# Expert inputs gathered in plain float32 by scaled one-hot matrices, four experts at a time, ahead of the experts that use them

## The chip, the core and the metric

The kernel runs on one core of one Trainium2 chip. A core has a tensor engine (TensorE, PE in the rows, its weight loads PEld), a vector engine (VectorE, DVE), a scalar engine (ScalarE, ACT), GpSimd (POOL) and SyncE (SP), whose queue issues most of the transfers. Matrix products are written to PSUM, in banks of 512 float32 per partition; all else lies in SBUF. The metric is the device time of one execution in microseconds (us), the median of several runs; lower is better.

## What is computed

A state-space block is followed by a transformer of two layers (`DEPTH_2 = 2`). The change touches only the feed-forward part of these two layers, in which each of 16 experts picks the 32 of 256 tokens that it rates highest:

```python
def expert_choice_ffn(h, w_router, w1, w3, w2):
    B, T, _ = h.shape
    cap = (EC_CAPACITY_FACTOR * T) // N_EXPERTS          # 32
    aff = jax.nn.softmax((h @ w_router).astype(jnp.float32), axis=-1)
    gate, idx = lax.top_k(jnp.swapaxes(aff, 1, 2), cap)
    bidx = jnp.arange(B)[:, None, None]
    xe = h[bidx, idx]
    hid = jax.nn.silu(jnp.einsum('becd,edf->becf', xe, w1)) * jnp.einsum('becd,edf->becf', xe, w3)
    ye = jnp.einsum('becf,efd->becd', hid, w2) * gate[..., None].astype(h.dtype)
    return jnp.zeros_like(h).at[bidx, idx].add(ye)
```

Here `h` is `rms_norm(x) * (1 + scale) + shift`. In layer 0 this runs on two streams with the same weights, `x` and the context `xc`; in layer 1 on `x` alone. All of `w1`, `w3` and `w2` is 1024 x 1024 float32 per expert, so an expert has 12 MB of weights, and a layer 192 MB.

## The kernel before

`moe(l, streams, stk)` holds the feed-forward of one layer; `ns` is the number of streams, 2 in layer 0 and 1 in layer 1. Its `run()` goes over the experts `e = 0..15` (called expert 0 to 15 here).

**One expert.** `ffn` (L1282) multiplies the expert's gathered inputs by a weight matrix: four tiles `wm` of 1 MB, two blocks `k` of 128 input channels each. In layer 0 one `k` is two products of 64 output columns x 512 (64 = 32 tokens of each stream); they stand in different column halves of the array. In layer 1 one `k` is four products of 32 x 256. The first `ffn` gives `p1`, the second `p3`; `hid` = silu(p1) * p3 is transposed on TensorE (`ps_t`), copied to `hidT`, and the third `ffn` multiplies `hidT` by `w2` into `py`. VectorE multiplies that by `g2` into `ye` (L1349). Every four experts, `gates` builds a matrix `PgT` of gate values, and eight products `ps_b<-ye,PgT` scatter the four experts' outputs back; VectorE adds them to `x` and `xc` (L1361). This is called the combine.

**The gather.** The inputs `xe` of an expert are 1024 channels x 32 tokens, by channel in partitions. `chosen` (L1203) builds a one-hot matrix P (token x chosen slot) by comparing the rank `POS` with `iota1`. `gather(s, part, k)` (L1213) then makes block `k` of stream `s` for all experts of a `part`: the tokens are scaled by `QS` (the 1/rms of each token) and split into two float32r tiles `xp` (ScalarE L1227, VectorE L1228), four products with P add up in one PSUM bank, and `affine` (L160) writes the block to `xe`, ScalarE and VectorE in turn, as (1 + scale) and shift. In layer 0 the parts are experts 0-3, 4-7 and 8-15 (`PARTS`, L1196), in layer 1 four times four experts. There is one buffer of `xp` for the late parts, and in layer 0 two PSUM banks `ps_g` for gathers.

**Order.** The first part is gathered inside expert 0 (`first`); the others are a list `late`, of which `more` takes one item at each of 14 places of an expert. A scheduler of the framework then reorders instructions within engines, by its own simulated times; what stands on an engine is read from the built program, below.

**Weight buffers.** `load_m` (L1268) issues the transfers of `wm` on SP's queue, in the order of use. Each takes the next buffer of a list: 22 in the first round of layer 0 (18 common ones, L1519, and 4 that later become `ye` and the gathered inputs), 18 in each round after it. A transfer waits until the products that read the tile before it in the same buffer are done, and everything behind it on the queue waits too.

Of the kernel before, what the change touches and what calls it, by code (L numbers as in the profile page):

```python
# [113 lines left out]
def kernel(ctx, tc, A, out, dbg=None):  # L114
# [1055 lines left out]
    def moe(l, streams, stk):  # L1170
# [8 lines left out]
        def inputs(part):  # L1179

            if part in xe:
                return
            if part < 2:
                if ns == 2:
                    v = mp.tile([128, 2048], F32, name=("xe0", "xf0")[part])
                else:
                    v = xe["y"][:, 1024:2048] if part else mp.tile([128, 1024], F32, name="xe0")
                v = v.rearrange("p (k e w) -> p k e w", k=8, e=4)
                xe[part] = [v[:, k] for k in range(8)]
            else:  # L1190
                v = [mp.tile([128, 2048], F32, name=f"xf{ns - 1 + i}").rearrange("p (k e w) -> p k e w", k=8 // ns, e=8)
                     for i in range(ns)]
                xe[part] = [v[k * ns // 8][:, k % (8 // ns)] for k in range(8)]


        PARTS = [(0, 4), (4, 4)] + ([(8, 8)] if ns == 2 else [(8, 4), (12, 4)])  # L1196
# [14 lines left out]
        pair = {}  # L1211

        def gather(s, part, k, n=1):  # L1213

            if k % n == 0:
                c = in_pairs(k) if n == 1 else slice(128 * k, 128 * k + 128 * n)
                if n == 1:
                    xp = mp.tile([128, 2, 2, 128], F32R, name="xp")  # L1220
                    h, o = pair[s] = [xp[:, i] for i in range(2)]
                else:
                    h, o = pair[s] = [rowp.tile([128, 512], F32R, name="xp", tag="r").rearrange("p (t c) -> p t c", t=2)
                                      for i in range(2)]
# [4 lines left out]
            e0, ne = PARTS[part]  # L1229
            ps = ps_("g" if ns == 2 else "a")[:, 0:32 * ne].rearrange("p (e w) -> p e w", w=32)  # L1230
# [4 lines left out]
            o = xe[min(part, 2)][k][:, e0 % 8 if part > 1 else 0:][:, :ne]  # L1235
            affine(o[:, :, 32 * s:32 * s + 32], ps, MS[:, i_sc, k, s:s + 1], shift[:, k, s:s + 1])
# [57 lines left out]
        def run():  # L1294
            if ns == 1:
                acc = [psb() for j in range(4)]
# [4 lines left out]
            inputs(0)  # L1301
            P0 = mp.tile([128, ns, 2, 4, 32], F32R, name="P0", tag="P")
            for s in range(ns):
                chosen(s, 0, P0[:, s])

            def first(k):
                for s in range(ns):
                    gather(s, 0, k, 2)
# [556 lines left out]
```

## Time and profile before

| | |
|---|---|
| Median of 3 runs | 1884.86 us (1883.54 to 1889.22) |
| The profiled execution's own time | 1879.31 us |
| Its span, first to last instruction | 1877.3 us |
| Mean granted TensorE clock | 0.928 of full |
| PE, DVE, ACT, POOL busy | 87%, 42%, 28%, 18% of the span |
| HBM read | 554.18 MB, 296 GB/s over the span |
| The chain that ended last | PE 59%, DMA 27%, DVE 7%, ACT 3% |

The span has a first part up to the router of layer 0 (about 755 us), the first expert stage (layer 0, to about 1230 us), layer 1's mixer, and the second expert stage from about 1428 us to the end. The shares are means over stages with different limits. The chain is followed back from the last instruction, at each step to what released it. PEclk is the granted clock, 1.00 for 2.4 GHz and 0.50 for 1.2 GHz. A plain float32 product leaves two records of the same shape in the trace, a float32r product one. A line number is often that of a helper: L149 is every matrix product, L255 every transpose.

### The profile page before, as it was taken

How to read it: one execution, taken by the hardware profiler on the slowest of the kernel's cores; microseconds unless marked ns; L12 is line 12 of the kernel's file. 1: busy time of each engine (PE TensorE's matmuls, PEld its weight loads, DVE VectorE, ACT ScalarE, POOL GpSimd, SP SyncE). 2: the span in 40 equal slices, each digit the busy share in tenths (PEclk: the TensorE clock that was granted, in tenths of full speed). 3: DMA queues.
4: the chain of work that ended last, by engine and by line, in shares of the span. 5: the costliest groups of instructions: out<-in, count | busy, mean ns of one | idle time of the engine just before them, and what ended most of it. 6: DMA issues, size and time to landing. Idle time of an engine off the chain costs nothing.

```text
span 1877.3 us, 29103 instructions
## 1 busy us (share of the span) xinstructions
PE 1642.5 (87%) x12038; PEld 1039.4 (55%) x12038; DVE 788.9 (42%) x1566; ACT 517.8 (28%) x1042; POOL 335.3 (18%) x291
## 2 busy tenths in 40 slices
PE   5999999999999999999989999889997976766665
PEld 4787877889888777433333333258775532222221
DVE  3538889957555665332232121164654410000002
ACT  4334545636444442211110000062442300000001
POOL 4104544733423411000000000031310000000001
PEclk8999999999999999899989999999997987777777
DMA  9567544646576639889969999962187999999996
GB/s 348 189 223 232 167 143 145 201 152 212 179 233 169 228 125 396 313 352 420 421 269 420 421 421 421 420 214 78 68 362 271 423 425 425 425 425 425 425 424 261
DMA packets 173192, 557.13 MB, mean 297 GB/s; under 512 B 22579, under 2 KB 79271, under 8 KB 124164
## 3 DMA queue, kind: packets, MB, share of 16 engines
q1 hardware_dynamic: 166688, 547.92, 75.5%
q10 hardware_dynamic: 5732, 6.33, 1.0%
q8 instruction: 95, 1.56, 0.3%
q0 software_dynamic: 640, 1.02, 0.1%
q14 instruction: 37, 0.30, 0.0%
HBM read 554.18 MB, written 1.05 MB: 296 GB/s over the span
## 4 chain that ended last, share of the span: by engine, by line
PE 59%; DMA 27%; DVE 7%; ACT 3%; issue 2%; POOL 1%; SPq 0%; DVEq 0%; POOLq 0%; ACTq 0%
PE ps_a L149 47%; DMA wm<-in_moe_w_dram 22%; PE ps_b L149 7%; PE ps_b L255 3%; DMA w<-in_w_in_dram 2%; PE ps_g L149 1%; DVE w L827 1%; DMA w<-in_even_w_in_dram 1%; DMA w<-in_w_ada_dram 1%; ACT wh L203 1%; DVE wh L205 1%; DMA w<-in_even_w_out_dram 1%; DVE ye L1349 1%; DVE hid L1331 1%; PE ps_t L255 1%
## 5 line engine op out<-in xcount | busy, mean ns | idle before, releaser
L149 PE MATMUL ps_a<-wm,xf 128*32 128x256 f32 (+1 forms) x1792 | 277.5, 557 | 61.7 <-DMA wm<-in_moe_w_dram 60.3
L149 PE MATMUL ps_a<-wm,hidT 128*32 128x256 f32 (+1 forms) x1536 | 207.2, 509 | 42.0 <-DMA wm<-in_moe_w_dram 25.3
L149 PEld LDWEIGHTS ps_a<-wm,xf 128*32 128x32 f32 (+1 forms) x1792 | 92.5, 138 | 236.3 <-issue 143.3
L203 ACT ACTIVATE wh<-w 128x1024 fp32r<-128x1024 f32 (+3 forms) x152 | 151.6, 1007 | 171.8 <-PE ps_a L149 92.3
L205 DVE TENSOR_TENSOR wh<-w,wh 128x1024 fp32r<-128x1024 f32 (+3 forms) x102 | 135.4, 1331 | 86.5 <-ACT wh L203 86.2
L205 POOL TENSOR_TENSOR wh<-w,wh 128x1024 fp32r<-128x1024 f32 (+3 forms) x50 | 115.0, 2300 | 311.9 <-ACT wh L203 287.8
L1331 DVE TENSOR_TENSOR hid<-hid,ps_a 128x512 f32<-128x512 f32 (+1 forms) x32 | 17.7, 554 | 346.5 <-PE ps_a L149 346.5
L149 PEld LDWEIGHTS ps_a<-wm,hidT 128*32 128x32 f32 (+1 forms) x1536 | 71.3, 131 | 149.2 <-issue 76.5
L1349 DVE TENSOR_TENSOR ye<-ps_a,SC 32x512 f32<-32x512 f32 (+1 forms) x128 | 70.8, 553 | 179.4 <-PE ps_a L149 177.9
L149 PE MATMUL ps_a<-hT,wh 128*128 128x512 f32 (+1 forms) x672 | 138.2, 362 | 5.8 <-ACT hT L522 4.3
L1248 POOL TENSOR_TENSOR Pg<-Pg,BC 128x128 f32<-128x128 f32 x24 | 9.5, 422 | 735.1 <-DVE Pg L1246 735.1
L1329 ACT ACTIVATE hid<-ps_a 128x512 f32<-128x512 f32 (+1 forms) x32 | 15.7, 490 | 448.8 <-PE ps_a L149 448.8
L149 PEld LDWEIGHTS ps_a<-hT,wh 128*128 128x128 f32 x672 | 112.1, 199 | 25.7 <-ACT hT L522 4.7
L149 PE MATMUL ps_a<-E,wh 128*128 128x256 f32 x768 | 103.7, 291 | 6.2 <-DVE wh L205 2.3
L149 PE MATMUL ps_a<-wm,xe 128*32 128x256 f32 (+1 forms) x768 | 105.1, 486 | 0.7 <-ACT hid L1329 0.5
L149 PE MATMUL ps_a<-wh,E 128*128 128x256 f32 (+1 forms) x576 | 101.9, 327 | 3.1 <-ACT wh L203 1.9
L149 PEld LDWEIGHTS ps_a<-E,wh 128*128 128x128 f32 x768 | 96.7, 194 | 12.5 <-ACT E L476 2.6
L149 PEld LDWEIGHTS ps_a<-wh,E 128*128 128x128 f32 x576 | 82.0, 189 | 17.0 <-issue 4.8
L641 DVE SCALAR_TENSOR_TENSOR acc<-ps_a,CV,acc 128x189 f32<-128x189 f32 (+2 forms) x160 | 66.6, 427 | 5.1 <-ACT acc L630 2.5
L1050 ACT ACTIVATE pr<-ps_a,nb 128x512 f32<-128x512 f32 (+1 forms) x80 | 47.8, 599 | 75.4 <-DVE nb L1047 64.5
L149 PE MATMUL ps_a<-w,SC 128*32 128x128 f32 x1728 | 64.2, 283 | 2.5 <-DMA w<-in_w_ada_dram 2.0
L149 PE MATMUL ps_a<-wm,ye 128*32 128x256 f32 x512 | 45.4, 498 | 23.0 <-DMA wm<-in_moe_w_dram 23.0
(526 smaller groups left out, 2419.5 us busy)
## 6 DMA issues: line engine op xcount, KB each, us to landing
wm<-in_moe_w_dram SPq DMA_DIRECT2D x382, 1024.0 KB, 19.5
w<-in_ada_w_dram SPq DMA_DIRECT2D x46, 1024.0 KB, 6.7
w<-in_even_w_in_dram SPq DMA_DIRECT2D x24, 1024.0 KB, 6.7
w<-in_w_ada_dram SPq DMA_DIRECT2D x12, 1024.0 KB, 8.4
w<-in_w_in_dram SPq DMA_DIRECT2D x8, 1024.0 KB, 8.5
w<-in_even_w_out_dram SPq DMA_DIRECT2D x8, 1024.0 KB, 6.9
w<-in_w_in_dram SPq DMA_DIRECT2D x12, 512.0 KB, 6.3
w<-in_w_in_dram SPq DMA_DIRECT2D x8, 768.0 KB, 4.3
```

The lines of the kernel that those rows point to most:

```text
L149: PE.matmul(o, l, r, start=start, stop=stop, **kw)
L203: S.activation(hv, wv, AF.Copy)
L205: (G if flip_lo[0] == 0 else V).tensor_tensor(lo, wv, hv, op=OP.subtract)
L255: PE.transpose(o, i, ident[:n, :n])
L641: V.scalar_tensor_tensor(o, xi[:, r0 + dr:r1 + dr, c0 + dc:c1 + dc], tap(i, j), o, op0=OP.mult, op1=OP.add)
L827: V.scalar_tensor_tensor(w[:, r], cb[:, c, 1], dt[:, c, 24 + h:25 + h], w[:, r], op0=OP.mult, op1=OP.add)
L1050: S.activation(pr[:, :n], ps[:, :n], AF.Exp, bias=nb, scale=scale, accum_out=su)
L1248: G.tensor_tensor(g_, g_, bcast(AFF[s][:, t, e4, None], [128, 4, 32]), op=OP.mult)
L1329: S.activation(hid, p1[:, :N], AF.Silu)
L1331: V.tensor_tensor(hid, hid, p3[:, :N], op=OP.mult)
L1349: V.tensor_tensor(ye[o:o + 32, s, N * j:N * j + N], py[i:i + 32, :N], G2[i:i + 32, :], op=OP.mult)
```

## The change

The one-hot matrix P is now plain float32 and holds the token's scale: VectorE compares (`tensor_tensor`) and then multiplies by `QS` (`tensor_scalar`), for both streams in one `chosen` call. `gather` multiplies `x` or `xc` itself by it, in two plain float32 products in place of four float32r ones; the tiles `xp` and the instructions that fill them are gone. All parts have four experts, so layer 0 has four parts of 16 gathers instead of two of 16 and one of 16 that were twice as wide. The order of `late` is parts 1, 3, 2 in layer 0, with the streams in turn, at 0.8 item per place; part 2 starts at expert 4, into the buffer of part 0. In layer 0 `ye` has two buffers, and the combine of experts 0-3 moves from the end of expert 3 to that of expert 5.

```diff
-        def chosen(s, part, P):
-            e0, n = PARTS[part]
-            Ps[s] = P
+        def chosen(part):
+            inputs(part)
+            P = mp.tile([128, ns, 2, 4, 32], F32, name="P", tag="P")
+            for s in reversed(range(ns)):
+                Ps[s, part] = P[:, s]
+                for t in range(2):
+                    V.tensor_tensor(P[:, s, t], bcast(iota1[:, None, :], [128, 4, 32]),
+                                    bcast(POS[s][:, t, 4 * part:4 * part + 4, None], [128, 4, 32]), op=OP.is_equal)
+                    V.tensor_scalar(P[:, s, t], P[:, s, t], QS[s][:, t:t + 1], None, op0=OP.mult)
+        def gather(s, part, k):
+            ps = ps_("g" if ns == 2 else "a")[:, 0:128].rearrange("p (e w) -> p e w", w=32)
             for t in range(2):
-                V.tensor_tensor(P[:, t], bcast(iota1[:, None, :], [128, n, 32]),
-                                bcast(POS[s][:, t, e0:e0 + n, None], [128, n, 32]), op=OP.is_equal)
...
-                for t in range(2):
-                    q = QS[s][:, t:t + 1]
-                    S.activation(h[:, t], streams[s][:, t, c], AF.Copy, scale=q)
-                    V.scalar_tensor_tensor(o[:, t], streams[s][:, t, c], q, h[:, t], op0=OP.mult, op1=OP.subtract)
...
-            for t in range(2):
-                for i in range(2):
-                    c = slice(0, 128) if n == 1 else in_pairs(k % n)
-                    mm(ps, pair[s][i][:, t, c], Ps[s][:, t], start=t == 0 and i == 0, stop=t == 1 and i == 1)
+                mm(ps, streams[s][:, t, in_pairs(k)], Ps[s, part][:, t], start=t == 0, stop=t == 1)
+            affine(xe[part][:, k, :, 32 * s:32 * s + 32], ps, MS[:, i_sc, k, s:s + 1], shift[:, k, s:s + 1])
...
-            late = [(s, part, k) for part in range(1, len(PARTS)) for s in range(ns) for k in range(8)]
+            late = [(s, part, k) for part in ((1, 3, 2) if ns == 2 else (1, 2, 3)) for k in range(8) for s in range(ns)]
+            turn = [0.0]
...
             def more(_):
-                if late:
+                if late and not (ns == 2 and late[0][1] == 2 and e < 4) and e > 0:
+                    turn[0] += 0.8
+                    if turn[0] >= 1.0:
+                        turn[0] -= 1.0
...
-                if e % 4 < 3:
+
+                qt = (e + 1) // 4 - 1 if ns == 1 or e > 5 else 0
+                if e % 4 < 3 and (ns == 1 or e != 5) or ns == 2 and e == 3:
                     continue
-                PgT = gates(e // 4)
+                assert ns == 1 or not late
+                PgT = gates(qt)
```

What stands on TensorE before and after is shown at three places, each first before and then with the change; `x4` is a count of products in a row. The first is layer 0 from the third `ffn` of expert 2 on (`ps_g` are gathers).

```order
L149 MATMUL ps_a<-wm,hidT 64x512 x13
L149 MATMUL ps_g<-P,xp 128x128
L149 MATMUL ps_a<-wm,hidT 64x512
L149 MATMUL ps_g<-P,xp 128x128 x3
L149 MATMUL ps_a<-wm,hidT 64x512 x2
L149 MATMUL ps_a<-wm,xe_7695 64x512 x11
L149 MATMUL ps_g<-P,xp 128x128
L149 MATMUL ps_a<-wm,xe_7695 64x512
L149 MATMUL ps_g<-P,xp 128x128 x3
L149 MATMUL ps_a<-wm,xe_7695 64x512 x15
L149 MATMUL ps_g<-P,xp 128x128 x4
L149 MATMUL ps_a<-wm,xe_7695 64x512 x5
```

```order
L149 MATMUL ps_a<-wm,hidT 64x512 x13
L149 MATMUL ps_g<-P,x 128x128 x2
L149 MATMUL ps_g<-P,xc 128x128 x2
L149 MATMUL ps_a<-wm,hidT 64x512 x3
L149 MATMUL ps_a<-wm,xe 64x512 x11
L149 MATMUL ps_g<-P,x 128x128 x2
L149 MATMUL ps_g<-P,xc 128x128 x2
L149 MATMUL ps_a<-wm,xe 64x512 x14
L149 MATMUL ps_g<-P,x 128x128 x2
L149 MATMUL ps_g<-P,xc 128x128 x2
L149 MATMUL ps_a<-wm,xe 64x512 x7
L149 MATMUL ps_g<-P,x 128x128 x2
```

Gathers, which stood in pieces of one, three or four products of four-product gathers, now stand in pairs of one gather of `x` and one of `xc`, and there are twice as many of them in an expert.

The second place is the end of expert 5 in layer 0: the last rows of its third `ffn` and what follows.

```order
L149 MATMUL ps_a<-wm,hidT 64x512 x2
L149 MATMUL ps_g<-P,xp 128x256 x12
L149 MATMUL ps_b<-ye,PgT 128x512
L149 MATMUL ps_g<-P,xp 128x256
L149 MATMUL ps_b<-ye,PgT 128x512
L149 MATMUL ps_g<-P,xp 128x256 x3
L149 MATMUL ps_b<-ye,PgT 128x512
```

```order
L149 MATMUL ps_g<-P,xc 128x128 x2
L255 MATMUL ps_t<-kb,hid 128x128 x4
L149 MATMUL ps_a<-wm,hidT 64x512 x12
L255 MATMUL ps_b<-kb,Pg 128x128 x4
L149 MATMUL ps_a<-wm,hidT 64x512 x4
L149 MATMUL ps_a<-wm,xe 64x512 x4
L149 MATMUL ps_b<-ye,PgT 128x512 x3
L149 MATMUL ps_a<-wm,xe 64x512 x8
L149 MATMUL ps_b<-ye,PgT 128x512 x3
L149 MATMUL ps_a<-wm,xe 64x512 x8
L149 MATMUL ps_b<-ye,PgT 128x512 x2
L149 MATMUL ps_a<-wm,xe 64x512 x12
```

Before, 28 products of gathers and five of the combine stand ahead of expert 6's first product (the seven rows go on in the same way up to it). With the change no gather is left there; eight products of the combine stand inside the first `ffn`s of expert 6.

The third is the start of the second expert stage (layer 1), behind the last product of the router.

```order
L149 MATMUL ps_b<-sel,ones 128x16
L149 MATMUL ps_a<-P_11544,xp 128x128 x8
L149 MATMUL ps_a<-wm,xe_11543 32x256 x4
L149 MATMUL ps_a<-P_11544,xp 128x128 x8
L149 MATMUL ps_a<-wm,xe_11543 32x256 x4
L149 MATMUL ps_a<-P_11544,xp 128x128 x4
```

```order
L149 MATMUL ps_b<-sel,ones 128x16
L149 MATMUL ps_a<-P,x 128x128 x6
L149 MATMUL ps_a<-wm,xe 32x256 x4
L149 MATMUL ps_a<-P,x 128x128 x2
L149 MATMUL ps_a<-wm,xe 32x256 x4
L149 MATMUL ps_a<-P,x 128x128 x2
```

Six products of three gathers now stand ahead of expert 0's first product, where eight of two gathers stood, and two ahead of the second, where eight stood. The order on SP's and POOL's queues is the same before and after.

## Rows read from the trace of the kernel before

**Rows 1.** Chain of waits that ended last: start us, us, what (xinstructions).
```profile
1163.47 10.34 PE ps_a L149 x47
1173.81 19.79 DMA wm<-in_moe_w_dram
...
1213.57 1.96 PE ps_a L149 x8
...
1483.47 19.81 DMA wm<-in_moe_w_dram
...
1842.23 18.32 DMA wm<-in_moe_w_dram
```

**Rows 2.** Stretches of 10 us: busy time by engine, PEclk, DMA share, GB/s.
```profile
810.00:820.00 10.00, 9.50 (x44) 4.00 (x44) 2.98 (x7) 1.76 (x5) 0.00 (x0) 1.00 0.77 277
...
830.00:840.00 10.00, 10.00 (x44) 3.38 (x44) 1.80 (x6) 2.72 (x7) 0.00 (x0) 1.00 1.01 427
...
950.00:960.00 10.00, 6.96 (x22) 3.62 (x20) 8.16 (x16) 3.02 (x8) 0.00 (x0) 0.84 0.04 13
960.00:970.00 10.00, 9.18 (x34) 2.92 (x36) 3.88 (x7) 0.02 (x1) 0.00 (x0) 0.75 0.43 162
980.00:990.00 10.00, 10.00 (x50) 3.43 (x48) 2.75 (x4) 0.00 (x0) 0.00 (x0) 1.00 1.02 425
```

**Rows 3.** Waits of the DMA queue (SPq), 835 to 1000 us: total, times, longest.
```profile
SPq L1279 <- PE ps_a L149: 124.8, 56, 21.7
```

**Rows 4.** Timeline of TensorE in the first expert stage: start us, us, instructions.
```profile
815.59 6.22 PE L149 MATMUL ps_a<-wm,hidT 128*64 128x512 f32 x26 [0.18 <-DVE hidT L158]
...
828.42 1.07 PE L149 MATMUL ps_a<-wm,xe 128*64 128x512 f32 x2
...
842.64 6.22 PE L149 MATMUL ps_a<-wm,hidT 128*64 128x512 f32 x26 [0.22 <-ACT hidT L156]
...
871.04 6.22 PE L149 MATMUL ps_a<-wm,hidT 128*64 128x512 f32 x26
...
888.80 2.84 PE L149 MATMUL ps_b<-ye,PgT 128*128 128x512 f32 x6
...
942.35 1.07 PE L149 MATMUL ps_g<-P,xp 128*128 128x256 f32 x4
...
958.43 1.01 PE L149 MATMUL ps_g<-P,xp 128*128 128x256 f32 x3 [1.81 <-DVE xp L1228]
960.82 15.97 PE L149 MATMUL ps_a<-wm,xf 128*64 128x512 f32 x64 [1.38 <-DVE ye L1349]
...
979.09 7.09 PE L149 MATMUL ps_a<-wm,hidT 128*64 128x512 f32 x32 [0.69 <-ACT hidT L156]
...
1002.34 8.78 PE L149 MATMUL ps_a<-wm,hidT 128*64 128x512 f32 x32 [0.83 <-issue]
```

**Rows 5.** Timeline of TensorE, two runs of eight records.
```profile
662.45 1.05 PE L149 MATMUL ps_b<-KV,prT 128*128 128x128 f32 x8
...
772.64 1.17 PE L149 MATMUL ps_g<-P,xp 128*128 128x128 f32 x8 [0.20 <-ACT xe L163]
```

**Rows 6.** Weight loads by form: busy us, mean ns, idle before and releaser.
```profile
L149 PEld LDWEIGHTS ps_b<-KV,prT 128*128 128x128 f32 x288 | 35.9, 191 | 6.4 <-issue 4.9 <-ACT pr L1050 0.7 <-DVE mx L1045 0.3
...
L149 PEld LDWEIGHTS ps_g<-P,xp 128*128 128x128 f32 x192 | 30.0, 209 | 41.2 <-issue 29.4 <-ACT xp L1227 6.7 <-DVE xp L1228 3.9
```

**Rows 7.** VectorE by form: busy us, mean ns, idle before and releaser.
```profile
L1208 DVE TENSOR_TENSOR P<-kb 128x128 fp32r<-128x128 f32 x16 | 6.5, 449 | 6.3 <-PE ps_g L149 6.2
...
L486 DVE TENSOR_SCALAR w<-w 128x192 f32<-128x192 f32 x1 | 0.3, 261 | 0.4 <-ACT w L485 0.4
```

**Rows 8.** Timeline of TensorE at the start of the second expert stage.
```profile
1427.82 1.94 PE L149 MATMUL ps_a<-P,xp 128*128 128x128 f32 x8 [0.70 <-DVE P L1208]
1429.88 1.08 PE L149 MATMUL ps_a<-wm,xe 128*32 128x256 f32 x8
...
1441.04 5.80 PE L149 MATMUL ps_a<-wm,xe 128*32 128x256 f32 x88
```

More of the change, by code (lines that the diff above doesn't have):

```diff
@@ L1179, in inputs @@
         def inputs(part):
[L1181 to L1189, printed above, removed]
-            else:
[L1191 to L1196, printed above, removed]
+            if ns == 2:
+                v = mp.tile([128, 2048], F32, name="xe", tag=("xe0", "xf0", "xe0", "xf1")[part])
+            elif part == 0:
+                v = mp.tile([128, 1024], F32, name="xe", tag="xe0")
+            elif part == 1:
+                v = xe["y"][:, 1024:2048]
+            else:
+                if part == 2:
+                    xe["f"] = mp.tile([128, 2048], F32, name="xf", tag="xf0")
+                v = xe["f"][:, 1024 * (part - 2):1024 * (part - 1)]
+            xe[part] = v.rearrange("p (k e w) -> p k e w", k=8, e=4)
         Ps = {}
@@ L1294, in run @@
         def run():
+            yes = {}
             if ns == 1:
@@ L1299, in work @@
                 return rowp.tile([128, 512], F32, name=name, tag="r")[:, :n]
[L1301 to L1304, printed above, removed]
+            chosen(0)
+            late = [(s, part, k) for part in ((1, 3, 2) if ns == 2 else (1, 2, 3)) for k in range(8) for s in range(ns)]
+            turn = [0.0]
             def first(k):
-                for s in range(ns):
-                    gather(s, 0, k, 2)
-            late = [(s, part, k) for part in range(1, len(PARTS)) for s in range(ns) for k in range(8)]
+                if k < 7:
+                    for s in reversed(range(ns)):
+                        gather(s, 0, k + 1)
             def more(_):
-                if late:
-                    s, part, k = late.pop(0)
-                    if k == 0:
-                        inputs(min(part, 2))
-                        chosen(s, part, mp.tile([128, 2, PARTS[part][1], 32], F32R, name="P", tag="P"))
-                    gather(s, part, k, 3 - ns)
+                if late and not (ns == 2 and late[0][1] == 2 and e < 4) and e > 0:
+                    turn[0] += 0.8
+                    if turn[0] >= 1.0:
+                        turn[0] -= 1.0
+                        s, part, k = late.pop(0)
+                        if part not in xe:
+                            chosen(part)
+                        gather(s, part, k)
+            for s in reversed(range(ns)):
+                gather(s, 0, 0)
             first(0)
@@ L1323, in xk @@
                 def xk(k):
-                    return xe[0 if e < 4 else 1 if e < 8 else 2][k][:, e % (8 if e >= 8 else 4)]
+                    return xe[e // 4][:, k, e % 4]
                 hook = more if e else first
@@ L1329, in run @@
                 S.activation(hid, p1[:, :N], AF.Silu)
-                p3 = ffn(xk, A["moe_w3_2"][l, e], more if e and 0 else None)
+                p3 = ffn(xk, A["moe_w3_2"][l, e])
                 V.tensor_tensor(hid, hid, p3[:, :N], op=OP.mult)
@@ L1339, in run @@
                 py = ffn(lambda K: hidT[:, K % nblk, W * (K // nblk):W * (K // nblk) + W], A["moe_w2_2"][l, e],
-                         more if e and 1 else None, last=e == 15)
+                         more, last=e == 15)
                 if e == 0:
                     gate2()
-                    yq = xe["y"] = mp.tile([128, 2048], F32, name="ye")
-                    ye = yq.rearrange("p (s n) -> p s n", s=2)
+                if e == 0 or ns == 2 and e % 4 == 0:
+                    xe["y"] = mp.tile([128, 2048], F32, name="ye", tag=("ye", "xf2")[e // 4 % 2])
+                    ye = yes[e // 4] = xe["y"].rearrange("p (s n) -> p s n", s=2)
                 o = 32 * (e % 4)
@@ L1356, in run @@
                             ps = acc[2 * t + h] if ns == 1 else psb()
-                            mm(ps, PgT[:, 256 * s + 128 * t:256 * s + 128 * t + 128], ye[:, s, 512 * h:512 * h + 512],
+                            mm(ps, PgT[:, 256 * s + 128 * t:256 * s + 128 * t + 128],
+                               yes[qt if ns == 2 else 0][:, s, 512 * h:512 * h + 512],
                                start=ns > 1 or e == 3, stop=ns > 1 or e == 15, skip_group_check=ns == 1)
```

14 lines of the change are left out of this document (removed).

## Prediction

> **What bounds the kernel now.** I read the chain of waits first, since it tells what ended last in each stage. Near the end of the first expert stage TensorE hands over to the transfers of expert weights at 1173.81 us, and they hold the chain up to 1213.57; in the second expert stage they hold it from 1483.47 to past 1842.23 [rows 1]. So both expert stages end when their last weights arrive, and a gain must come from transfers that run earlier, not from less work. Next I read the DMA share by stretches: at full rate it is 1.00 to 1.01 and 425 to 427 GB/s, so a tile of 1.0486 MB takes 2.47 us. It was 0.77 at 810 us, full at 830, 0.04 from 950 to 960 and 0.43 from 960 to 970, and full again behind that [rows 2]. Those holes are the time that can be won. What the queue waits for there is products into `ps_a`, which must be done with a tile before its buffer is loaded again [rows 3]. So I read TensorE's timeline at the hole: expert 5's third `ffn` is over at 942.35, then come only gathers and the combine, some of them waiting (1.81 us for `xp`, 1.38 us for `ye`), and expert 6 starts at 960.82 [rows 4]. For 18.5 us no buffer came free. Its first 64 records then took 15.97 us, where two runs of 32 take 14.2, and the mean granted clock of that stretch was 0.75 [rows 2, 4]: its first tile, 1.8 us at full clock, was done at about 960.8 + 3.6 = 964.4.
>
> **A rule for the end of the stage.** Tile m (12 per expert) frees the buffer of tile m + 18. If it is done at time c, the transfers from there to tile 191 end no earlier than c + (174 - m) x 2.47. The largest such value over m is the stage's end. Before, expert 6's first tile (m = 72) gives 964.4 + 251.9 = 1216.3, close to where the chain leaves the transfers. Expert 1's third `ffn` (m = 20), whose run begins at 815.59, is the earlier candidate: 815.6 + 1.8 + 154 x 2.47 = 1197.8. The 18.5 us between the two is all that filling the second hole could give while experts 0 and 1 keep their pace.
>
> **The change part by part.**
>
> *The burst.* All 28 gather products ahead of expert 6 go, and the combine moves into expert 6. What remains is how late the gathers make the experts that now carry them. I measure from the third `ffn` of one expert to that of the next. Without a gather it is 1002.34 - 979.09 = 23.25 us. Before, from expert 1 to 2 it is 27.05 with 17 gather records, from 2 to 3 28.40 with 19 [rows 4]; at four records a gather that is 8.95 us over nine gathers, 0.99 each, with the broken runs around them. With the change there are 10 gathers in each of the three intervals from expert 1 to 4, and 8 in that from 4 to 5.
>
> *The price of a gather, p.* Two plain float32 products leave four records, as four float32r products did. The trace has no plain float32 gather; the nearest row is attention's product of 128 x 128 weights with 128 columns, eight records in 1.05 us, where eight records of the old gather took 1.17 [rows 5]. So the low end is 0.53 a gather. The high end is the 0.99 above. Between them I add up the interval from expert 2 to 3 as it now stands on TensorE. Two products in different halves of the array share a slot of 7.09/8 = 0.886 us, but an odd run leaves one alone (two records, 1.07) [rows 4]. The runs 13, 3, 11, 14, 7 make 7 + 2 + 6 + 7 + 4 = 26 slots, 23.0 us. Three pairs of gathers in the open, each 1.05 plus 0.1 for the switch, are 3.5. Around the transposes TensorE idles anyhow: 23.25 less 24 slots (21.3) is 2.0, which two pairs and the transposes now fill and overrun to about 3.0. With 0.1 at the start of each of four runs the sum is 29.9. The other three intervals come to 30.5, 31.4 and 28.9 in the same way; the mean over 38 gathers is p = 0.73. For the two intervals of before the same sum gives 28.6 and 29.2, so it is 0.8 to 1.5 too long; taking 1.0 off each interval gives 0.63. I take p = 0.68.
>
> *The stage's end.* The third `ffn` of expert 5 begins at 815.6 + 4 x 23.25 + 38p. That of expert 6 comes 32.1 us later: 24 slots (21.3), eight combine products (three took 2.84, so 7.4 with their switches) [rows 4], four transposes for `PgT` (0.7) and the pause and switches (2.7). Its first tile (m = 80) is done 1.8 later and 94 tiles follow, 232.2 us. The end is 1174.7 + 38p: 1200.5 at 0.68, and 15.8 earlier than 1216.3. At 0.53 expert 1's bound of 1197.8 holds instead (18.5 earlier); at 0.99 it is 1212.3 (4.0 earlier). Expert 7 and later have no gathers, at most a combine, and each value of the rule falls by some 6 us an expert.
>
> *Expert 0.* Its gathers have 64 records as before. It loses the waits for `xp` and gains two multiplications of P ahead of the first product; a multiplication of 192 columns took 0.26 us [rows 7]. I take -0.7, between -2 (a gather less of waiting at each end) and +1. It moves all that follows.
>
> *Work on other engines.* 112 instructions on ScalarE and 112 on VectorE go, 24 multiplications and 16 `affine` come. In the stage these engines are not what the transfers wait for, except in the burst, counted above; I cost this at nothing. If the cover failed, a new P (eight instructions, four comparisons of 0.45 and four multiplications of some 0.26, 2.8 us) [rows 7] would hold up the gather behind it at three places. In the program P stands behind the last gather that reads the old one, and one run of `ffn` products lies between; eight products take 3.5 us.
>
> *The second expert stage.* Here the combine and the order of the late gathers matter little: from 1483.47 the transfers are the chain [rows 1] and TensorE only has to start early. The first tiles need 32 gather records before and after. Eight took 1.94 us at the start [rows 8], against 1.17 elsewhere [rows 5]. P is ready two multiplications later, 0.5 us. If plain records also ran at double their 0.131, they would take 0.26 instead of 0.24, 0.6 us over 32. I take +0.5, between -1 and +1.1.
>
> **The sum.** -15.8 - 0.7 + 0.5 = **-16.0 us**. Against the profiled execution (1879.31, span 1877.3 and 2.0 around it) that is 1863.3. The runs shown have their median 5.5 us above it, so I forecast 1884.86 - 16 = **1869 us**.
>
> **The rivals.**
> *A, the forecast:* p between 0.53 and 0.9, gain 10 to 19 us.
> *B, hidden in the pace of experts 1 to 5:* twice as many gathers, each at the old 0.99, leave 4 us of the 16, and the time is about 1881. For it speaks that 0.99 is measured here; against it that pairs break half as many runs per gather.
> *C, slower:* the gathers wait for their two PSUM banks. In the burst seven gathers, of twice the width, took 18.5 us less 4.7 for five combine products and 1.4 for `ye`, 1.8 each [rows 4]. Half way between that and 0.99, at p = 1.4, the stage would end at 1227.9, 11.6 later, and the time would be about 1896; from p = 1.1 on nothing is won. For it: the pairs on both sides of a transpose use both banks twice within 2 us. Against it: the waits of the burst were for `xp`, which is gone, and most pairs stand a run of products apart.
> *F, slower weight loads:* plain float32 weights could lose a fast path that float32r ones had. If each of the 152 records of the 38 gathers took one load (0.19 us) more, p would be 1.44 and the time about 1897. Against it: the old gather's loads took 209 ns as a mean, attention's plain ones 191 [rows 6]. The Trainium skill (TensorE: Matmul & The Clock Gate, Weight-path perf modes) says that Fast Weight Load is on for 128 weights unless the input is FP32, and also that it wins nothing for fp32. By its first half F would hold; the rows side with its second half.
> *D, more:* expert 0 and 1 also run faster and open the bound of 1197.8; 4 to 8 us more, about 1863.
> *E, nothing moves:* the hole returns as several small ones because TensorE stays the slower side from expert 1 to 6; its size is that of B.
>
> **How the numbers follow.** A 0.66, B with E 0.14, C 0.08, F 0.02, D 0.10. About 0.3% (5.7 us) is what a measurement can tell here. A and D are faster; B and E fall within 0.3%; C and F are slower. That makes faster 0.77, same 0.13, slower 0.10. The range of A alone is 1866 to 1875; to hold 8 in 10 it reaches from D's middle to B: 1862 to 1882.
>
> **What would show it.** Right: no stretch from 850 us on with a DMA share below 0.9 in the first expert stage, expert 6 starting near 943, its combine inside its first `ffn`, third `ffn`s of experts 1 to 5 some 29 to 30 us apart, the second expert stage as long as before. Wrong: intervals of 33 us or more, waits of gathers on `affine` or P, a DMA share of 0.8 to 0.9 through experts 2 to 5, or a hole at expert 4, where the inputs of part 2 reuse the buffer of part 0.

## The result and the profile after

The median fell from 1884.2 us (four runs, 1877.76 to 1889.22) to 1861.1 us (four runs, 1860.97 to 1864.59): a ratio of 0.9884, with a 95% interval of 0.9851 to 0.9916. The prediction was 1869 us in a range of 1862 to 1882, with 0.77 on faster. So the direction and the main place were right, and the gain of 23 us was 7 us larger than the 16 forecast. The new median lies 0.9 us below the range. The ratio's interval stands for a gain of 15.8 to 28.1 us, which just holds the forecast; that the gain is larger is seen in the stage lengths below. The profiled execution took 1860.97 us, with a span of 1859.1 us.

The chain of waits of the changed kernel, to be read beside [rows 1] (start us, us, what):

```profile
1029.68 9.88 PE ps_a L149 x46
...
1039.58 16.58 DMA wm<-in_moe_w_dram
...
1196.83 1.96 PE ps_a L149 x8
...
1474.52 19.49 DMA wm<-in_moe_w_dram
```

TensorE hands over to the transfers at 1039.58 instead of 1173.81, and the stage's last weights are there at 1196.83 instead of 1213.57. Stretches of 10 us of the changed kernel, columns as in [rows 2]:

```profile
810.00:820.00 10.00, 10.00 (x56) 4.77 (x53) 2.02 (x4) 0.92 (x2) 0.00 (x0) 1.00 0.83 323
...
830.00:840.00 10.00, 10.00 (x50) 3.96 (x48) 2.09 (x9) 1.51 (x3) 0.00 (x0) 1.00 1.00 405
...
950.00:960.00 10.00, 9.82 (x42) 2.90 (x38) 1.44 (x3) 0.60 (x1) 0.00 (x0) 1.00 1.01 419
960.00:970.00 10.00, 8.55 (x34) 3.05 (x36) 0.63 (x1) 0.60 (x1) 0.00 (x0) 0.83 1.01 419
```

The hole is gone: from 830 us to the end of the stage no stretch has a DMA share under 1.00. The longest single wait of the DMA queue for a product between 835 and 1000 us, 21.7 us before [rows 3], is 5.5:

```profile
SPq L1258 <- PE ps_a L149: 131.8, 67, 5.5
```

TensorE's timeline in the first expert stage, beside [rows 4]: the starts of the third products of experts 1 to 6, and the start of expert 6 with its combine.

```profile
814.92 6.22 PE L149 MATMUL ps_a<-wm,hidT 128*64 128x512 f32 x26
...
844.90 6.22 PE L149 MATMUL ps_a<-wm,hidT 128*64 128x512 f32 x26
...
872.91 6.22 PE L149 MATMUL ps_a<-wm,hidT 128*64 128x512 f32 x26
...
902.46 6.22 PE L149 MATMUL ps_a<-wm,hidT 128*64 128x512 f32 x26
...
930.35 5.37 PE L149 MATMUL ps_a<-wm,hidT 128*64 128x512 f32 x24 [0.75 <-ACT hidT L156]
...
938.01 1.89 PE L149 MATMUL ps_a<-wm,xe 128*64 128x512 f32 x8
939.83 2.84 PE L149 MATMUL ps_b<-ye,PgT 128*128 128x512 f32 x6
...
962.20 8.78 PE L149 MATMUL ps_a<-wm,hidT 128*64 128x512 f32 x32 [0.77 <-ACT hidT L156]
```

Expert 6 starts at 938.01, with its combine cut into pieces between its products, and not at 960.82. The intervals from expert 1 to 5 are 29.98, 28.01, 29.55 and 27.89 us.

The start of the second expert stage, beside [rows 8]:

```profile
1413.84 0.64 PE L149 MATMUL ps_b<-sel,kb 128*128 128x32 f32 x2 [0.28 <-DVE sel L1162]
...
1415.88 2.93 PE L149 MATMUL ps_a<-P,x 128*128 128x128 f32 x12 [1.01 <-DVE P L1208]
1418.74 1.08 PE L149 MATMUL ps_a<-wm,xe 128*32 128x256 f32 x8
...
1420.42 0.64 PE L149 MATMUL ps_a<-wm,xe 128*32 128x256 f32 x8
...
1425.38 4.98 PE L149 MATMUL ps_a<-wm,xe 128*32 128x256 f32 x88
```

Eight records of weight products take 1.08 us once and 0.64 from 1420.42 on; before, they took 1.08 throughout, until the run of 88 that began at 1441.04. This the prediction did not have.

**Reading the gain by stages.** The program's parts that no edit touches do not repeat to the microsecond: over the twelve profiled executions of this study the `sel` product of the first layer comes between 750.8 and 760.9 us, and from the end of the first expert stage to the second layer's `sel` it takes 212.6 to 217.5 us. A gain of 4 us drowns in that. So I read each expert stage by itself, from its `sel` product: the first to the end of its last transfer in the chain, the second to the end of the span.

| kernel | first stage | second stage | median, us | ratio to before (95%) |
|---|---|---|---|---|
| before | 460.0 | 451.2 | 1884.2 | |
| after | 439.6 | 445.3 | 1861.1 | 0.9884 (0.9851 to 0.9916) |
| l0_only | 441.4 | 449.2 | 1864.1 | 0.9897 (0.9865 to 0.9929) |
| l1_only | 459.3 | 445.1 | 1881.8 | 0.9983 (0.9966 to 0.9999) |
| plain_only | 447.0 | 445.3 | 1867.2 | 0.9898 (0.9875 to 0.9922) |
| f32r_sched | 451.3 | 449.3 | 1877.3 | 0.9944 (0.9923 to 0.9965) |
| combine_e3 | 445.5 | 445.8 | 1866.5 | 0.9915 (0.9894 to 0.9936) |
| double_gather | 468.2 | 446.3 | 1887.3 | 1.0019 (1.0002 to 1.0037) |
| no_late | 438.4 | 445.7 | 1860.6 | 0.9886 (0.9864 to 0.9908) |
| dummy_plain | 441.8 | 446.9 | 1867.7 | 0.9910 (0.9878 to 0.9942) |
| dummy_f32r | 441.7 | 451.5 | 1871.2 | 0.9914 (0.9883 to 0.9946) |
| filler | 440.0 | 444.6 | 1856.9 | 0.9862 (0.9835 to 0.9890) |

A stage of one form repeats within 2.2 us. The first stage is 459.7 us with the gathers of before (mean of 2) and 440.9 with the change (mean of 5: after, l0_only, dummy_plain, dummy_f32r, filler): 18.8 less. The second one is 449.9 with the old gathers (mean of 3: before, l0_only, f32r_sched) and 445.6 with plain ones (mean of 6: after, l1_only, plain_only, combine_e3, double_gather, no_late): 4.3 less. Together 23.1 us, as much as the medians differ by. That the two agree to a tenth is chance, since a stage repeats within 2.2 us and the medians less closely.

### The profile page after: what moved, and what is told of

It reads as the page before. It is cut to its first block, busy times and chain, and to the rows that moved or that the text cites. A ratio compares the mean times of both kernels' runs of the same rounds, so it can differ in the third digit from the quotient of the medians.

```text
span 1859.1 us, 29008 instructions
## 1 busy us (share of the span) xinstructions
PE 1628.6 (88%) x12102; PEld 1038.2 (56%) x12102; DVE 754.7 (41%) x1490; ACT 481.1 (26%) x938; POOL 335.4 (18%) x291
## 4 chain that ended last, share of the span: by engine, by line
PE 54%; DMA 33%; DVE 7%; ACT 3%; issue 2%; POOL 1%; SPq 0%; POOLq 0%; DVEq 0%; ACTq 0%
PE ps_a L149 42%; DMA wm<-in_moe_w_dram 28%; PE ps_b L149 6%; PE ps_b L255 3%; PE ps_g L149 2%; DMA w<-in_w_in_dram 2%; DMA w<-in_even_w_in_dram 2%; DVE w L827 1%; ACT wh L203 1%; DVE wh L205 1%; DMA w<-in_w_ada_dram 1%; DMA w<-in_even_w_out_dram 1%; DVE acc L641 0%; DVE wh L786 0%; DVE ye L1333 0%
## 5 line engine op out<-in xcount | busy, mean ns | idle before, releaser
L149 PE MATMUL ps_a<-wm,xe 128*64 128x512 f32 (+1 forms) x1536 | 267.9, 526 | 2.8 <-DMA wm<-in_moe_w_dram 2.8
L149 PE MATMUL ps_a<-wm,hidT 128*32 128x256 f32 (+1 forms) x1536 | 212.7, 524 | 41.8 <-DMA wm<-in_moe_w_dram 24.2
L149 PEld LDWEIGHTS ps_a<-wm,xe 128*64 128x64 f32 (+1 forms) x1536 | 89.4, 128 | 152.5 <-issue 129.5
L149 PE MATMUL ps_a<-wm,xf 128*32 128x256 f32 x1024 | 96.7, 514 | 57.9 <-DMA wm<-in_moe_w_dram 57.9
L149 PEld LDWEIGHTS ps_a<-wm,xf 128*32 128x32 f32 x1024 | 34.9, 136 | 119.0 <-DMA wm<-in_moe_w_dram 68.9
```

The source lines that it names most:

```text
L149: PE.matmul(o, l, r, start=start, stop=stop, **kw)
```

## The experiments

Theory 1 is the prediction's: the gain is made where the burst ahead of expert 6 held up the transfers, and the rule for tiles and buffers gives the stage's end. Theory 2 says that part of the gain is the second stage's, through TensorE's clock. Theory 3 says that the plain products by themselves are the whole gain, and their spreading is worth nothing.

### l0_only and l1_only: the change in one stage at a time

Both forms of `moe` stand in the kernel, `moe_o` of before and `moe_n` of the change, and each layer calls its own. l0_only (in l1_only the two are exchanged):

```
-    run, gts, xf, slots = moe(0, [x, xc], ms)
+    run, gts, xf, slots = moe_n(0, [x, xc], ms)
...
-    run, gts, xf, slots = moe(1, [x], ms)
+    run, gts, xf, slots = moe_o(1, [x], ms)
```

> The change in the first expert stage alone; the second expert stage keeps the gathers of before. Theory 1 (as predicted: the gain is made in the first expert stage, the second one is worth 0.5 us) expects the time of the changed kernel, 1861 us, within 2 us, and the second stage from its last sel product to the end as long as in the changed kernel's trace, 445 us. Theory 2 (plain products ahead of the second stage also bring it some 6 us) expects 1867 us, with 451 us from sel to the end, TensorE at half clock until some 15 us into the stage.

> The change in the second expert stage alone; the first one keeps the gathers of before. Theory 1 expects the kernel before, 1884 us, within 2 us, with the hole in the transfers just ahead of expert 6's products back (DMA share under 0.5 in one stretch of 10 us near 960). Theory 2 expects 1878 us: 6 us less, all of it after the second stage's sel product, and the hole as well.

l0_only took 1864.06 us and l1_only 1881.76. The first lies between the two theories and its interval holds both. The second's interval is 0.2 to 6.4 us under before and reaches both as well. The stage lengths decide: 449.2 us for the second stage with its old gathers, 445.1 with the new ones, whatever the first stage does. In l1_only the hole is back; its stretches, columns as in [rows 2]:

```profile
950.00:960.00 10.00, 8.46 (x23) 4.56 (x24) 5.80 (x16) 3.79 (x11) 0.00 (x0) 0.83 0.56 232
960.00:970.00 10.00, 6.13 (x22) 2.49 (x22) 9.55 (x17) 1.27 (x4) 0.00 (x0) 0.87 0.01 2
```

l0_only's start of the second stage on TensorE:

```profile
1416.21 1.94 PE L149 MATMUL ps_a<-P,xp 128*128 128x128 f32 x8 [0.70 <-DVE P L1208]
1418.27 1.08 PE L149 MATMUL ps_a<-wm,xe 128*32 128x256 f32 x8
...
1427.36 1.08 PE L149 MATMUL ps_a<-wm,xe 128*32 128x256 f32 x8
...
1429.42 7.14 PE L149 MATMUL ps_a<-wm,xe 128*32 128x256 f32 x88
```

The runs of eight stay at 1.08 us, as in the kernel before. So theory 1's step "second stage +0.5" is wrong, and most of the gain, 18.8 of 23.1 us, is the first stage's.

### plain_only and f32r_sched: the products and the schedule apart

plain_only puts plain products by a scaled one-hot matrix into the old parts, order, rate and combine:

```
         def chosen(s, part, P):
...
+                V.tensor_scalar(P[:, t], P[:, t], QS[s][:, t:t + 1], None, op0=OP.mult)
...
-                for i in range(2):
...
-                    mm(ps, pair[s][i][:, t, c], Ps[s][:, t], start=t == 0 and i == 0, stop=t == 1 and i == 1)
+                mm(ps, streams[s][:, t, in_pairs(k)], Ps[s][:, t], start=t == 0, stop=t == 1)
```

> The kernel before with plain float32 gathers by scaled one-hot matrices, but with its old parts (the last eight experts in one gather), its old rate of one gather per product pair and its combine at the end of expert 3. Theory 1: four of the 16 eight-wide gathers and the combine fall between the third products of experts 3 and 4, with all the late gathers done by then. With 0.59 us for a four-wide gather, 1.1 us for an eight-wide one and 8.6 us for a combine the intervals of third products from expert 0 on are 26.8, 30.2, 34.3 and 36.3 us, so expert 4's third products start 127.6 us after expert 0's, near 913, and the rule (118 tiles of 2.50 us behind them) ends the stage near 1210 us, 9 us after the changed kernel's: 1870 us for the kernel. Theory 3 (the plain products are the whole gain, the spreading is worth nothing) expects 1861 us; a theory in which the spreading is the whole gain expects 1880 us or more.

f32r_sched keeps all of the change but puts the rounded pairs back:

```
-                V.tensor_scalar(P[:, s, t], P[:, s, t], QS[s][:, t:t + 1], None, op0=OP.mult)
...
-                mm(ps, streams[s][:, t, in_pairs(k)], Ps[s, part][:, t], start=t == 0, stop=t == 1)
+                for i in range(2):
...
+                    mm(ps, pair[s][i][:, t, c], Ps[s, part][:, t], start=t == 0 and i == 0, stop=t == 1 and i == 1)
```

> The changed kernel's parts, order, rate, two result tiles and later combine, but with the rounded float32r pairs of before (four products a gather, their operands made by ScalarE and VectorE, one pair tile for the late ones). The compiler's order for it leaves four to five gathers to each of experts 0 to 4 and ten or more to experts 5 and 6, with the combine in expert 8. Theory 1: those late ones have slack (92 tiles behind expert 7's third products, which come at some 975 us, end the stage near 1181), so only the slower start through experts 0 and 1 counts (4.4 us), and the second stage starts as before (3 to 6 us): 1866 to 1872 us, most of the gain kept. Theory 3 (plain products are the gain) expects 1880 us or more.

plain_only took 1867.2 us (1870 expected) and its first stage 447.0: 12.7 of the 18.8 us come with the plain products alone. What it lacks is the spreading. The intervals of third products from expert 0 on were 30.87, 29.61, 31.98 and 33.46 us (26.8, 30.2, 34.3 and 36.3 expected), and its last hole lies where the combine is, ahead of expert 4's third products:

```profile
910.00:920.00 10.00, 9.25 (x42) 3.55 (x44) 2.07 (x3) 0.60 (x1) 0.00 (x0) 1.00 0.85 319
```

f32r_sched took 1877.3 us where theory 1 expected at most 1872: a miss. Its second stage is 449.3, as theory 2 has it. Its first stage, 451.3, keeps 8.4 of the 18.8 us. I had put expert 7's third products at 975 us; they came at 1001.64, and expert 8's, the ones that bind, at 1038.01. From expert 0 to 9 its 46 gathers added 271.49 - 235.53 = 36.0 us over the kernel without late gathers, 0.78 each, where the plain ones of the changed kernel added 23.9 us, 0.52 each. I had also left a combine out of that sum, 8.9 us by the kernel without late gathers (32.17 - 23.25). Four float32r products a gather come apart into odd runs of 1 and 3 between the weight products. They waited 1.2 us in all for `xp`, so it is not the operands' making. And the compiler put so many of them off that the transfers waited at the end, in experts 7 and 8 (stretches as in [rows 2]):

```profile
1000.00:1010.00 10.00, 9.68 (x46) 4.30 (x48) 5.88 (x16) 3.42 (x10) 1.71 (x4) 1.00 0.88 331
...
1020.00:1030.00 10.00, 10.00 (x34) 2.73 (x32) 3.19 (x5) 0.60 (x1) 0.00 (x0) 1.00 0.78 293
1030.00:1040.00 10.00, 8.24 (x39) 3.11 (x40) 2.07 (x3) 0.00 (x0) 0.00 (x0) 1.00 0.90 324
```

So theory 3 falls in part: neither half gives the whole, and the products are the larger half.

### combine_e3: the combine left at the end of expert 3

All 48 late gathers must then be done by the end of expert 3, so they are also made faster, at 1.15 for each place instead of 0.8, and part 2 gets a buffer of its own (in lines that are not shown):

```
-                    turn[0] += 0.8
-                    if turn[0] >= 1.0:
+                    turn[0] += 1.15 if ns == 2 else 0.8
+                    while late and turn[0] >= 1.0:
...
-                if e == 0 or ns == 2 and e % 4 == 0:
+                if e == 0:
...
-                qt = (e + 1) // 4 - 1 if ns == 1 or e > 5 else 0
+                qt = e // 4
```

> The changed kernel with one result tile and the combine of experts 0 to 3 left at the end of expert 3, so all 48 late gathers are made at a rate of 1.15 for each product pair instead of 0.8. Theory 1: the compiler's order puts 8, 10, 10, 10 and 8 gathers and the combine (in two pieces, in experts 4 and 5) between the third products of experts 0 to 5; at 0.59 us and 8.6 us expert 5's third products start near 938 and the stage ends near 1204 us, 3 us after the changed kernel's: 1864 us (1861 to 1869). A rival by which the later combine is what removes the hole expects the old hole of the transfers back and 1875 us or more.

1866.5 us, and 445.5 for the first stage, 4.6 more than with the change (3 expected). Expert 5's third products came at 942.97 (938 expected). The only stretch after 840 us with a DMA share under 0.95 is 940 to 950, at 0.80. The old hole does not come back: once the gathers are cheap and spread, the late combine is worth about 5 us, together with the slower rate of the gathers that it allows; the run does not part the two.

### double_gather: each gather's products twice

```
-            for t in range(2):
+            for t in range(2 if ns == 1 else 4):
+                t = t % 2
                 mm(ps, streams[s][:, t, in_pairs(k)], Ps[s, part][:, t], start=t == 0, stop=t == 1)
```

> The changed kernel with the two products of each gather of the first expert stage issued twice, the second pair over the first (same result). A gather then costs some 1.18 us of TensorE. Theory 1: between the third products of experts 0 to 6 lie 5, 9, 12, 10 and 10 gathers and the combine, and the first 16 gathers make expert 0 later by up to 9.4 us, so expert 6's third products start near 998 and the rule ends the stage near 1234 us, 33 us after the changed kernel's: 1894 us (1880 to 1900), slower than before. A rival by which gathers stand beside the transfers' pace and TensorE has slack expects no more than the later start, 1861 to 1871 us.

1887.3 us, as slow as before or slightly slower, and 468.2 us for the first stage, 27.3 over the change's (33 expected). From expert 1 to 5 the intervals grew by another 20.2 us. They hold 39 gathers here, one more than in the changed kernel; less 0.6 us for that one, the second pair of products costs 0.50 us a gather. TensorE's timeline shows the third products of expert 5 at 956.37 and of expert 6 at 987.75 (998 expected):

```profile
956.37 7.09 PE L149 MATMUL ps_a<-wm,hidT 128*64 128x512 f32 x32 [0.75 <-ACT hidT L156]
...
987.75 7.09 PE L149 MATMUL ps_a<-wm,hidT 128*64 128x512 f32 x32 [0.75 <-ACT hidT L156]
```

The rule gives 987.75 + 1.8 + 232.2 = 1221.7 for the end, and it came at 1219.04. TensorE has no slack here while it carries gathers: their price decides.

### no_late: the 48 late gathers left out

Experts 4 to 15 of the first stage work on the inputs of experts 0 to 3.

```
-                    return xe[e // 4][:, k, e % 4]
+                    return xe[e // 4 if ns == 1 else 0][:, k, e % 4]
...
-            late = [(s, part, k) for part in ((1, 3, 2) if ns == 2 else (1, 2, 3)) for k in range(8) for s in range(ns)]
+            late = [(s, part, k) for part in (() if ns == 2 else (1, 2, 3)) for k in range(8) for s in range(ns)]
```

> The changed kernel without the 48 late gathers of the first expert stage: experts 4 to 15 of it work on the gathered inputs of experts 0 to 3, so the output is not the reference's. Theory 1: nothing is left to gain there, as the tiles freed by experts 0 and 1 already set the end; expert 1's third products come 3 to 6 us sooner (floor near 1196), the tiles of expert 0 still end the stage near 1200 us: 1856 to 1861 us. A rival by which the late gathers still bound the stage expects their 28 us off, 1835 to 1845 us.

1860.6 us and 438.4 for the first stage: leaving out all 48 gathers, 24 us of TensorE's time, wins 2.5 us, hardly more than the 2.2 by which stages of one form differ. The third products of experts 1 and 2 on TensorE:

```profile
816.87 7.09 PE L149 MATMUL ps_a<-wm,hidT 128*64 128x512 f32 x32 [0.75 <-ACT hidT L156]
840.19 7.09 PE L149 MATMUL ps_a<-wm,hidT 128*64 128x512 f32 x32 [0.90 <-issue]
```

23.32 us lie between them, the prediction's 23.25. Expert 1's tile (m = 20) gives 816.87 + 1.8 + 380.4 = 1199.1, and the end came at 1199.32. So the bound that the prediction named, the pace of experts 0 and 1, is where the changed kernel now stands: there expert 1's tile gives 1197.1 and expert 6's 1196.2.

### dummy_plain, dummy_f32r and filler: what brings the clock back

The first two have the change in the first stage only. dummy_plain adds unused plain products ahead of the second stage's old gathers:

```
+            for i in range(3):
+                ps = ps_("a")
+                for j in range(2):
+                    mm(ps[:, 0:128], streams[0][:, j, 128 * i:128 * i + 128], Pd, start=j == 0, stop=j == 1)
```

> The change in the first expert stage alone, and in the second one, with the rounded float32r gathers of before, six unused plain float32 products (x by an unscaled one-hot matrix, 128 columns each) ahead of the first gather. Read is the second stage's length from its sel product to the end: 449 to 451 us with float32r gathers and 445 to 446 us with plain ones in the runs so far. If plain float32 products themselves bring TensorE's full clock back, it is granted some 4 to 5 us after the first of them, the eight-record runs of weight products take 0.64 us instead of 1.08 us, and the stage is 447 us long in spite of the added 2.9 us. A rival by which the clock returns at a time that does not depend on the kind of product expects half clock until 13 us after the first product and 452 to 454 us.

dummy_f32r issues the first old gather four times over:

```
-            for t in range(2):
+            for t in list(range(2)) * (4 if part == 0 and k == 0 else 1):
```

> The control of the run with unused plain products: the second stage's first gather issued four times over (12 more float32r products, the same 12 records and 128 columns each). If the kind of product decides, TensorE stays at half clock until some 13 us after its first gather, and the stage is 452 to 454 us long from its sel product. If more work in one piece is enough, the clock returns early here too, and the stage is near 447 us.

In dummy_plain (first fence) the run of eight at 1423.05 already takes 0.64 us, and the stage is 446.9 us long (447 expected). In dummy_f32r (second fence) the runs stay at 1.08 through 1433.43, and the stage is 451.5:

```profile
1415.87 0.39 PE L255 MATMUL ps_b<-kb,aT 16*128 16x16 f32 x2 [3.90 <-DVE aT L1156]
...
1418.59 2.93 PE L149 MATMUL ps_a<-Pd,x 128*128 128x128 f32 x12 [1.01 <-DVE Pd L1306]
...
1423.05 0.64 PE L149 MATMUL ps_a<-wm,xe 128*32 128x256 f32 x8
```

```profile
1417.30 0.39 PE L255 MATMUL ps_b<-kb,aT 16*128 16x16 f32 x2 [4.57 <-DVE aT L1156]
...
1419.72 4.50 PE L149 MATMUL ps_a<-P,xp 128*128 128x128 f32 x20 [0.70 <-DVE P L1208]
1424.34 1.08 PE L149 MATMUL ps_a<-wm,xe 128*32 128x256 f32 x8
...
1433.43 1.08 PE L149 MATMUL ps_a<-wm,xe 128*32 128x256 f32 x8
...
1435.49 6.06 PE L149 MATMUL ps_a<-wm,xe 128*32 128x256 f32 x88
```

Both added twelve records of 128 columns, and TensorE was as busy in the one as in the other (6.4 of 6.4 us and 6.2 of 6.3 from the first of them on). So at this place the full clock came back early with plain products and not with float32r ones. One thing more differs, the wait of TensorE for the routing (`aT`) just ahead: 3.90 us in dummy_plain, 4.57 in dummy_f32r, and the same two values in all other kernels with plain and with float32r gathers here. No run holds that wait equal, so that the kind of product alone decides is not shown.

filler is the changed kernel with four unused plain products in TensorE's wait for the second layer's routing:

```
         for t in range(2):
             tr(p[:16, 128 * t:128 * t + 128], aff[:, t])
+        if l == 1:
+            d = ps_("a")
+            for i in range(4):
+                mm(d[0:32, 0:256], aff.rearrange("p t e -> p (t e)"), src[:, i // 2, 256 * (i % 2):256 * (i % 2) + 256])
```

> The changed kernel with four unused plain float32 products of 256 columns in the wait of TensorE for the last routing of the second layer, some 4 us in which it stands idle and a few us ahead of that stage's first gather. If plain products bring the clock back, the first gathers start at full clock (12 records in 1.8 us instead of 2.9 us) and the second stage is 443 to 444 us long from its sel product instead of 445.5 us; the time would be 1859 to 1860 us, too little to be told from the changed kernel's 1861 us in the time alone. A rival by which the short idle time behind the filler (under 4 us) takes the clock away again expects 445.5 us.

The full clock was there at `sel` and lost again behind it, in the first gathers; the run of eight at 1412.00 is back at 1.08:

```profile
1403.73 3.62 PE L149 MATMUL ps_a<-x,BC 128*32 128x256 f32 x8
...
1408.27 0.41 PE L149 MATMUL ps_b<-sel,kb 128*128 128x32 f32 x2 [0.28 <-DVE sel L1166]
...
1409.90 2.17 PE L149 MATMUL ps_a<-P,x 128*128 128x128 f32 x12 [1.01 <-DVE P L1212]
1412.00 1.08 PE L149 MATMUL ps_a<-wm,xe 128*32 128x256 f32 x8
```

The stage is 444.6 us long, 0.5 to 1.7 less than in the other kernels with plain gathers there, about half of what was expected. Its median, 1856.9, is the lowest of all. But its profiled execution reached the first `sel` 6 us earlier than that of the changed kernel, while the filler stands in the second layer, and the two ratios' intervals overlap. That it beats the changed kernel is not shown.

## Why the prediction came out as it did

**The burst and the rule** held. Expert 6 started at 938.01 ("near 943"), the step from expert 5's to expert 6's third products is 31.85 us (32.1), and the rule at 2.47 us a tile gives ends within 3.3 us of the chain's in six kernels: 1216.3 for 1213.5 before, 1197.1 for 1196.8 after, 1206.3 for 1203.1 in plain_only, 1212.7 for 1209.5 in f32r_sched, 1206.6 for 1205.4 in combine_e3, 1221.7 for 1219.0 in double_gather. It is 1 to 3 us high where a later expert binds, and within 0.3 where expert 1 does. As terms: 15.8 + 0.7 were forecast for the first stage, and 18.8 measured. With experts 0 and 1 at their old pace the rule would end the stage 62.1 + 1.8 + 380.4 = 444.3 us after `sel`, where 459.7 was before and 440.9 is now. So some 15.4 us are the burst's and some 3.4 those of experts 0 and 1, where 0.7 was forecast. That the 15.4 come so near the 15.8 is in part luck: the gathers were cheaper than forecast, and the rule had put the old end 2.8 us too late.

**The price of a gather** was mis-sized, 0.68 for 0.59: the intervals from expert 1 to 5 sum to 115.43 us, 22.4 over four times 23.25, by 38 gathers. That is inside the range given (0.53 to 0.99), and it alone brings the forecast's end for expert 6 from 1200.5 to 1197.1. Taken against no_late over experts 0 to 9 it is 0.52, and 0.50 for the second pair in double_gather, so the value lies near attention's row, 0.53 [rows 5].

**Expert 0 and 1** gained more than 0.7. In the changed kernel the first weight product follows `sel` by 4.26 us instead of 5.65, and expert 1's third products by 57.7 instead of 62.1. Part of that is the clock, which the prediction did not count here either. Before, the first eight weight records run at half clock:

```profile
759.14 3.68 PE L149 MATMUL ps_a<-wm,xe 128*64 128x512 f32 x8
...
763.83 1.94 PE L149 MATMUL ps_a<-wm,xe 128*64 128x512 f32 x8
```

In the changed kernel they take 1.94, and its trace is the most favourable of the five with this first stage: in the other four they take 1.94 to 3.00, and expert 1's third products follow `sel` by 58.1 to 59.3. So rival D's condition came true, the bound of expert 1 moved, and the end with it.

**The second stage** is the step that failed: +0.5 forecast, -4.3 measured. The prediction saw that the records there run at double their length ([rows 8] beside [rows 5]) and took that as given for the plain ones too. It was half clock, as this stretch of the kernel before shows:

```profile
1426.00:1436.00 10.00, 9.09 (x49) 6.16 (x49) 4.01 (x12) 3.07 (x7) 0.00 (x0) 0.50 0.09 19
```

With plain products the full clock came back at the second run of eight. From `sel` to that run of 88 it is 11.5 us instead of 14.95, and the run itself takes 4.98 instead of 5.80, together 4.2 us. The stage lengths of these two traces differ by 5.9, the means by 4.3, so the clock is most of it. From 1474.52 on the transfers are the chain, so an earlier start is kept to the end.

**The other engines** at nothing: right. A P multiplication took 0.279 us (0.26 estimated), and no product of experts 1 to 5 waited for P. These are VectorE's rows of the changed kernel by form:

```profile
L1206 DVE TENSOR_TENSOR P<-kb 128x128 f32<-128x128 f32 x24 | 5.6, 286 | 3.5 <-PE ps_a L149 2.1 <-PE ps_g L149 1.3
L1208 DVE TENSOR_SCALAR P<-P,misc 128x128 f32<-128x128 f32 x24 | 5.5, 279 | 0.0
```

**The rivals.** B's price of 0.99 did not come. C's waits on the two banks did not either: even double_gather's gathers waited 0.4 us in all between 800 and 990 us, for P. double_gather also bears out that at p = 0.59 + 0.50 = 1.1 nothing is left of the gain. F falls by the weight loads of the changed kernel, 204 and 201 ns beside the old 209 [rows 6]:

```profile
L149 PEld LDWEIGHTS ps_g<-P,xc 128*128 128x128 f32 x128 | 18.4, 204 | 8.1 <-issue 7.3 <-DVE xe L165 0.8
L149 PEld LDWEIGHTS ps_g<-P,x 128*128 128x128 f32 x128 | 18.4, 201 | 18.1 <-issue 17.9 <-DVE P L1208 0.3
```

These rows side with the second half of what the Trainium skill (TensorE: Matmul & The Clock Gate, Weight-path perf modes) says, that the fast load wins nothing for fp32; whether it was on for either kind, no row here shows. D had the time, about 1863, but only in part for its reason: experts 0 and 1 and the cheaper gathers gave 2.3 us over the 16.5 forecast for the first stage, where D said 4 to 8, and the other 4.8 come from the second stage, of which no rival spoke. That its number came out is luck. The chances of A and D add up to 0.76, not 0.77, and those of B and E are 0.14; nothing hangs on it.

## What to carry to other kernels

Where buffers circulate, write the end as "time at which tile m frees its buffer, plus the tiles still to come by their transfer time", and take the largest: it tells which expert binds, what a hole costs and when to stop (here 24 us of TensorE work left out win 2.5 us). Work that must be done beside a stream of transfers cost least here in small pieces in whole runs, spread from the start; cheap and spread gathers gave 18.8 us, cheap ones alone 12.7, spread ones alone 8.4 (in the compiler's order, which put many of them late). And where a row at the start of a stage runs at double its length elsewhere, ask what would end that before carrying it over to the new form.

## What the runs showed of the hardware

TensorE's return from 1.2 to 2.4 GHz went with the kind of product at the start of the second stage. At the same place in the program seven runs with plain float32 products there (after, l1_only, plain_only, combine_e3, double_gather, no_late, dummy_plain) had the full clock by the second run of eight records. Four with float32r products alone (before, l0_only, f32r_sched, dummy_f32r) stayed at half clock until the run of 88, 13 to 16 us behind the first gather, though no idle time over 0.2 us stands in TensorE's timeline in between. Their wait for the routing ahead of it was 0.67 us longer (4.57 for 3.90). A stretch of dummy_f32r, columns as in [rows 2]:

```profile
1427.00:1431.00 4.00, 4.00 (x25) 2.15 (x25) 1.21 (x3) 1.37 (x3) 0.00 (x0) 0.50 0.35 100
```

The Trainium skill (TensorE: Matmul & The Clock Gate, The HAM clock gate) lets the engine's being busy release the throttle and in that section makes no difference between kinds of product; at this place the rows do. The weight products between the gathers are float32 in both and did not bring it back by themselves in the four runs.

But float32r products as such do not keep the clock down. At the start of the first stage it was back some 8 us behind the first float32r gather (755.23 in the kernel before), where plain ones took 3 to 6 in the runs that have them there. And early in the kernel before, products of 256 columns with the float32r tile `wh` begin at half clock at 44.63, and from about 50 us on they have the full clock:

```profile
44.63 10.75 PE L149 MATMUL ps_a<-hT,wh 128*128 128x256 f32 x68 [2.45 <-ACT hT L522]
```

```profile
43.00:50.00 7.00, 5.37 (x25) 5.37 (x26) 7.00 (x16) 3.98 (x6) 2.93 (x2) 0.52 0.55 198
50.00:53.00 3.00, 3.00 (x27) 3.00 (x27) 1.61 (x2) 1.29 (x3) 0.00 (x0) 0.97 0.55 179
```

What held it back at the start of the second stage, no run here shows.

The price of a product does not follow from its records alone: four records a gather took 0.52 us on the way from expert 0 to 9 as two plain products, and 0.78 as four float32r ones, at nearly the same mean clock (0.99 and 1.00) and with equal weight loads (201 and 204 ns, and 202).
